# Output projection of two blocks at a time, FFN operands placed earlier, and 1/sqrt with its state in PSUM

## The chip, the cores and the metric

The kernel is one program on one core of a Trainium2 chip. The core has TensorE (matmuls, called PE in the profile, with its weight loads PEld), VectorE (DVE), ScalarE (ACT), GpSimd (POOL) and the DMA queues, which this kernel issues from SyncE (SP). The metric is the device time of one execution in microseconds; the median of three runs of the kernel before is 2169.43 us (2167.53 to 2169.79).

## The reference

One decoder layer on 2048 tokens of width 1024, in float32:

```
h    = rms_norm(x, norm1_g)
proj = h @ w_in                       # 1024 x 1536: u (512), xr (512), yr (512)
s5   = s5_mixer(u, ...)               # 32 groups, 64 complex states each, a scan over the sequence,
                                      # z = gelu(y);  z * sigmoid(z @ w_glu + b_glu)
lru  = rglru_mixer(xr, yr, ...)       # conv(4), gates, real scan, times gelu(yr)
mix  = concat(rms_norm(s5, s5_out_g), rms_norm(lru, lru_out_g))
x    = x + mix @ w_out                # 1024 x 1024
h2   = rms_norm(x, norm2_g)
x    = x + (silu(h2 @ w_gate) * (h2 @ w_up)) @ w_down     # 1024 x 2816 x 1024
out  = rms_norm(x, final_g)
```

## The kernel before

Tokens are cut into four blocks of 512 (`TB`, `NB`); features lie on partitions in chunks of 128. Every float32 product is made of three matmuls on rounded operands: an operand is split into `hi` (a cast on ACT) and `lo` (a subtraction on DVE or POOL), and `mm3` (line 214) accumulates hi x hi, hi x lo and lo x hi into one PSUM bank. A **unit** is 128 output columns of a projection: `Unit` loads its weights in parts of 128x512 into `wraw` (6 buffers) and splits them into `whi` (4 buffers) and `wlo` (5). A unit of eight chunks is 24 matmuls.

The stages, in the order of the work:

1. `in_tb(b)`, four times: the input projection of block b, its convolution, gates and real scan (the LRU group). The LRU output goes to DRAM (`lrud`, its 1/sqrt row to `rld`), the S5 input to `ub`.
2. S5, in two halves g of two blocks each: eight steps `s5_in`, `s5_scan`, `s5_out` a half on PE, DVE and POOL, through single `s_wr`, `s_wi`, `s_ta`, `s_tb` buffers, on the buffer `U` (tag `u8`), which goes to DRAM as `zb`.
3. `glu_tb(b)`: z of a block is loaded, GELU (`zgelu`), split into hi and lo (`zsplit`, lines 911 and 912), two units of 24 matmuls against `w_glu`, sigmoid and product, sum of squares, 1/sqrt (`SumSq.finish`, `rsqrt`, `spread`), and `mix`, which writes the normed and split operands of the output projection. The operands of even blocks lie in `areaH`, `areaL` (tiles `aH`, `aL`, pool Q), those of odd blocks in `actH`, `actL` (pool A). `zsplit` writes into the same places.
4. `out_tb(b)`: eight units against `w_out`; the sum with x (line 968), its square (ACT), the running sum of squares (POOL; DVE for block 3), the store to `x1d`; at the end a 1/sqrt row to `r2d`. The order is GLU 0, GLU 1, out 0, out 1, GLU 2, GLU 3, out 2, out 3.
5. The FFN in two halves p of two blocks, by a seven-product scheme over 2x2 blocks (`PRODS`). `combos(p, k)` loads two rows of `x1d` and the 1/sqrt row into the three `hx` buffers (lines 1053, 1055), norms them (line 1059) and forms four sums `ht`; `x_first(0)` splits them into the operand tiles, `LATE` ones through DRAM (`xcd`). Gate and up products are line 1184, the down projection line 1324. At the end the last norm.

**What sets the order.** The code gives each piece a time in the plan with `at(t, fn)`, in units near a microsecond (`PT` = 0.65 for three matmuls); `Plan.run` traces the pieces in the order of these times. The framework then gives each engine its instructions in an order in which operands are ready, earlier traced ones first, and a buffer is given again when its last reader is through. So a time in the plan is a priority, and buffers and readiness decide the rest. The pools lie one on the other: `open_d1` closes L, Q and S, and pool D1 (`hx`, `ht`, the operand tiles, `rd`, `ws`) takes their place; its first tiles, `hx`, lie where Q's `areaH` and `areaL` pieces lay. `open_d2` does the same with A and D2 behind the output projection.

**1/sqrt.** `rsqrt` (lines 221 to 236) takes four columns of sums and runs one scaling, two integer steps and three Newton rounds of three instructions, twelve DVE instructions on 128x4 elements, all in the SBUF tile `nv`. It runs 20 times: four times for the input norms, four for the LRU halves, four in GLU, four behind the output projection, four in the last norm. `aux("nm")` is a single PSUM bank.

Of the kernel before, what the change touches and what calls it, by code (L numbers as in the profile page):

```python
# [79 lines left out]
def build(tc, nc, I, O, ctx):  # L80
# [44 lines left out]
    x1d = dram("x1d", (DM, SEQ))  # L125
    r2d = dram("r2d", (SEQ,))
# [94 lines left out]
    def rsqrt(ss, n):  # L221

        w_ = ss.shape[-1]
        v = P.tile([128, 3, w_], F32, tag=f"nv{w_}", name="nv", bufs=2)
        ms, y, w = v[:, 0, :], v[:, 1, :], v[:, 2, :]
        DV.tensor_scalar(out=ms, in0=ss, scalar1=1.0 / n, scalar2=EPS, op0=ALU.mult, op1=ALU.add)

        DV.tensor_scalar(out=w.bitcast(I32), in0=ms.bitcast(I32), scalar1=1, scalar2=None, op0=ALU.logical_shift_right)
        DV.tensor_scalar(out=y.bitcast(I32), in0=w.bitcast(I32), scalar1=-1.0, scalar2=float(0x5F3759DF),
                         op0=ALU.mult, op1=ALU.add)  # L230
        for _ in range(3):
            DV.tensor_tensor(out=w, in0=y, in1=y, op=ALU.mult)
            DV.scalar_tensor_tensor(out=w, in0=w, scalar=-0.5, in1=ms, op0=ALU.mult, op1=ALU.mult)
            ins = DV.scalar_tensor_tensor(out=y, in0=w, scalar=1.5, in1=y, op0=ALU.add, op1=ALU.mult)
        last.setdefault("rs", getattr(ins, "ins", ins))
        return y

    class SumSq:
# [16 lines left out]
        def finish(self, dst=None):  # L255
# [4 lines left out]
            y = rsqrt(ps[:, 0:4], 128 * self.n)  # L260
# [3 lines left out]
        def spread(y, dst=None):  # L264
# [10 lines left out]
            dst = A.tile([128, TB], F32, tag="rs", name="rs", bufs=3)  # L275
# [334 lines left out]
    def in_tb(b, t0):  # L610
# [31 lines left out]
        at(ts + 9.0, lambda: cur.__setitem__("rs", SumSq.spread(rsqrt(cur["ss"], DM))))  # L642
# [225 lines left out]
    for g, (ts, dt) in enumerate(((ts0, 10), (tP1 - 10.0, 7))):  # L868
# [18 lines left out]
    def glu_tb(b, t0):  # L887
# [9 lines left out]
        def lload():  # L897
            cur["rl"] = lt("xq", (128, TB))
            cur["l"] = [lt("r", bufs=2) for _ in range(2)]
# [6 lines left out]

        def zsplit():
            zh, zl = pair(b)
# [10 lines left out]
        for uu in range(2):  # L919
# [3 lines left out]
            def prod(uu=uu, u=u):  # L923
                for i in range(2):
                    cur["ps", 2 * uu + i] = acc()
                    mm3(cur["ps", 2 * uu + i], u, [(4 * i + k, k) for k in range(4)],
                        *pair(b), True, True)
# [12 lines left out]
        t = t0 + 16 * PT  # L940

# [4 lines left out]
        for i, k in enumerate((4, 5, 6, 7)):  # L946
            at(max(t0 + 6.0, t2s) + 0.5 * i, lambda k=k: mix(k))
        at(t + 6.0, lambda: cur.__setitem__("rs", cur["ss"].finish()))
        for k in range(4):
            at(t + 7.0 + 0.5 * k, lambda k=k: mix(k))  # L950

    def out_tb(b, t0):
        cur = C[b]
        ss = SumSq(8, dv=b == NB - 1)
        for m in range(8):
# [572 lines left out]
```

## Time and profile before

| | us |
|---|---|
| median of three runs | 2169.43 (2167.53 to 2169.79) |
| profiled execution, its own time | 2175.18 |
| its span, first to last instruction | 2173.4 |
| TensorE busy | 1956.8 (90%) |
| DVE, POOL, ACT busy | 1244.8, 1042.6, 815.4 |
| last matmul of the output projection starts | 777.7 |
| first FFN matmul starts | 778.0 |

A row of a stretch reads: its bounds and length, then for each engine busy time and number of instructions, the granted TensorE clock, the share of the DMA engines and GB/s. A row of a group reads: line, engine, operation, out<-in, shapes, count, then busy time, mean ns of one, and idle time of the engine before it with what ended it. A wait reads: who waited for whom, total us, times, longest. A row of the timeline reads: start, length, engine, line, operation, count, and idle time before it. Matmuls overlap, so a row of one matmul is longer than its share of time. Some matmul records, a few per cent, can be missing.

### The profile page before, as it was taken

The numbers are of one execution on the slowest core, as the hardware profiler recorded it, in microseconds if no ns is written. First come the engines' busy times: TensorE is split into PE (matmuls) and PEld (weight loads), VectorE is DVE, ScalarE is ACT, GpSimd is POOL, SyncE is SP. The second block draws the span as 40 slices with busy tenths as digits, with TensorE's granted clock in tenths as the row PEclk, the third lists the DMA queues.
The fourth block names the chain that finished last, engine by engine and source line by source line (L and its number), as shares of the span: only waits on it lengthen the run. The fifth ranks groups of instructions, "written<-read, shape, count | busy, mean of one in ns | idle before, by whom it ended". The sixth has DMA issues, their size and how long they took to land.

```text
span 2173.4 us, 26158 instructions
## 1 busy us (share of the span) xinstructions
PE 1956.8 (90%) x8600; PEld 1564.3 (72%) x8600; DVE 1244.8 (57%) x1920; ACT 815.4 (38%) x1340; POOL 1042.6 (48%) x855
## 2 busy tenths in 40 slices
PE   6758989877898968899999989999999999999996
PEld 4536767666776756677777777777777788888785
DVE  5997658488856586444444464444444536554644
ACT  4534653563354342232332342232332344333331
POOL 1576236468834468545545552312313336544442
PEclk8968999988998989999999999999999999999998
DMA  7746998874772888644444574444443569854633
GB/s 293 218 153 190 297 248 273 226 179 142 226 209 94 257 264 279 200 146 146 160 146 143 172 235 134 149 131 136 145 131 126 189 224 317 279 184 135 232 102 102
DMA packets 264423, 413.61 MB, mean 190 GB/s; under 512 B 60736, under 2 KB 82528, under 8 KB 264288
## 3 DMA queue, kind: packets, MB, share of 16 engines
q1 hardware_dynamic: 264288, 411.95, 59.7%
q8 instruction: 67, 1.10, 0.2%
q14 instruction: 68, 0.56, 0.1%
HBM read 288.89 MB, written 122.96 MB: 189 GB/s over the span
## 4 chain that ended last, share of the span: by engine, by line
PE 55%; DVE 4%; DMA 4%; POOL 3%; issue 2%; ACT 1%; SPq 0%; POOLq 0%; DVEq 0%; ACTq 0%
PE gt L1184 9%; PE acc L1184 9%; PE y L1184 9%; PE v L1184 5%; PE nm L1184 5%; PE y L1324 4%; PE acc L1324 4%; PE gt L1324 4%; PE v L1324 2%; PE nm L1324 2%; PE acc L214 2%; DVE wlo L1024 1%; DMA ht<-xcd 1%; DVE hx L1059 1%; DMA wraw<-w_down 1%
## 5 line engine op out<-in xcount | busy, mean ns | idle before, releaser
L1197 POOL TENSOR_TENSOR t<-t 128x512 f32<-128x512 f32 x66 | 100.8, 1527 | 348.9 <-DVE t L1223 219.4
L214 PE MATMUL acc<-actH,whi 128*128 128x512 f32 x528 | 220.0, 418 | 43.5 <-DVE gy L710 12.1
L1023 ACT CAST whi<-ws 128x512 fp32r<-128x512 f32 x176 | 109.2, 621 | 346.9 <-PE y L1184 90.4
L214 PE MATMUL acc<-actL,whi 128*128 128x512 f32 x528 | 217.5, 413 | 18.8 <-DVE actL L294 17.8
L214 PE MATMUL acc<-actH,wlo 128*128 128x512 f32 x528 | 216.9, 412 | 6.9 <-DMA wlo<-wlc 6.9
L1024 DVE TENSOR_TENSOR wlo<-ht,whi 128x512 fp32r<-128x512 f32 x112 | 107.1, 957 | 126.3 <-ACT whi L1023 122.1
L214 PEld LDWEIGHTS acc<-actH,whi 128*128 128x128 f32 x528 | 105.9, 201 | 73.8 <-issue 24.8
L1023 ACT CAST whi<-ht 128x512 fp32r<-128x512 f32 x154 | 95.1, 619 | 169.9 <-PE nm L1324 69.5
L1024 DVE TENSOR_TENSOR wlo<-ws,whi 128x512 fp32r<-128x512 f32 x176 | 134.1, 762 | 33.7 <-ACT whi L1023 33.6
L1024 DVE TENSOR_TENSOR wlo<-wraw,whi 128x512 fp32r<-128x512 f32 x88 | 72.0, 818 | 142.2 <-ACT whi L1023 142.2
L1184 PE MATMUL y<-xh,whi 128*128 128x512 f32 x308 | 124.7, 405 | 16.2 <-ACT t L1216 12.0
L214 PEld LDWEIGHTS acc<-actL,whi 128*128 128x128 f32 x528 | 105.1, 199 | 46.7 <-DVE actL L294 24.7
L1024 POOL TENSOR_TENSOR wlo<-ht,whi 128x512 fp32r<-128x512 f32 x42 | 57.9, 1379 | 158.9 <-ACT whi L1023 158.9
L1184 PE MATMUL acc<-xh,wlo 128*128 128x512 f32 x308 | 122.3, 397 | 9.6 <-DVE wlo L1024 9.6
L214 PEld LDWEIGHTS acc<-actH,wlo 128*128 128x128 f32 x528 | 105.2, 199 | 30.6 <-DMA wlo<-wlc 7.4
L1184 PE MATMUL acc<-xh,whi 128*128 128x512 f32 x308 | 122.4, 397 | 4.6 <-ACT xh L1023 3.3
L1184 PE MATMUL y<-xl,whi 128*128 128x512 f32 x308 | 123.3, 400 | 3.5 <-DVE xl L1024 3.5
L1184 PE MATMUL y<-xh,wlo 128*128 128x512 f32 x308 | 123.3, 400 | 2.9 <-DVE wlo L1024 2.9
L1184 PE MATMUL acc<-xl,whi 128*128 128x512 f32 x308 | 122.2, 397 | 1.7 <-DVE xl L1024 1.7
L1184 PE MATMUL gt<-xh,whi 128*128 128x512 f32 x308 | 121.4, 394 | 0.0
L1184 PE MATMUL gt<-xh,wlo 128*128 128x512 f32 x308 | 121.3, 394 | 0.0
L1184 PE MATMUL gt<-xl,whi 128*128 128x512 f32 x308 | 121.2, 394 | 0.0
(416 smaller groups left out, 5308.0 us busy)
## 6 DMA issues: line engine op xcount, KB each, us to landing
td<-t SPq DMA_DIRECT2D x154, 256.0 KB, 2.2
ht<-td SPq DMA_DIRECT2D x154, 256.0 KB, 3.0
wraw<-w_down SPq DMA_DIRECT2D x99, 256.0 KB, 4.5
wraw<-w_in SPq DMA_DIRECT2D x96, 256.0 KB, 5.2
scd<-ws SPq DMA_DIRECT2D x88, 256.0 KB, 2.1
ws<-scd SPq DMA_DIRECT2D x88, 256.0 KB, 2.6
wlo<-wlc SPq DMA_DIRECT2D x72, 256.0 KB, 4.4
wraw<-w_out SPq DMA_DIRECT2D x64, 256.0 KB, 4.5
```

Source lines behind the costliest of these rows:

```text
L214: PE.matmul(ps, lhsT=part[w][:, kw % 4, :], rhs=r_(x(kx)), start=first and i == 0 and j == 0, stop=last and i == n - 1 and j == 2)
L1023: AC.copy(hi, raw)
L1024: eng.tensor_tensor(out=lo, in0=raw, in1=hi.bitcast(F32), op=ALU.subtract)
L1059: DV.scalar_tensor_tensor(out=cur[i], in0=cur[i], scalar=pc("g2", k + 4 * i), in1=cur["rs"], op0=ALU.mult, op1=ALU.mult)
L1184: PE.matmul(ps, lhsT=a[:, k, :], rhs=x, start=j in FIRST and k == 0 and i == 0, stop=k == 3 and i == 2, skip_group_check=True)
L1197: (DV if q == 0 else GP).tensor_tensor(out=g, in0=c, in1=g, op=ALU.mult)
L1324: PE.matmul(BK[p][i], lhsT=a[:, i, :], rhs=x, start=j in FIRST and s == 0 and v == 0, stop=s == NSL - 1 and v == 2, skip_group_check=True)
```

## The change

- **Pairs.** `out_pair(b0)` takes blocks 0 and 1 together, and then blocks 2 and 3: one `Unit` of weights serves both. Units go to the two `acc` and two `gt` banks in turn (`out_bank`). The order is (0,b0), (1,b0), (0,b0+1), (1,b0+1), then units 2 and up for both blocks in turn; for the first pair, units 6 and 7 come last, block 0 first, and 32 `PT` later in the plan.
- **GLU 2 and 3** are placed behind the first twelve units of pair 0, before its last four. Their z is split into a tile of tag `u8` (`zpair`) and no longer into the operand areas; all eight `mix` steps are placed by `tm`, behind units (7,0) and (7,1). Odd blocks load their LRU half into `ig` and `T` in place of `xq` and `r`.
- **S5's second half** is placed 16 later in the plan.
- **FFN operands.** `open_d1` and `x_first(0)` are placed 64 `PT` earlier, at the start of pair 2. `x1d` and `r2d` become two DRAM tiles each, one a pair.
- **Sums.** One running sum for each block of a pair (`sum`, `sumh`); block 2's additions go to DVE like block 3's; `rs` has two buffers in place of three.
- **1/sqrt.** Scaled sum, estimate and integer step live in the PSUM bank of the sums (`room`), one copy of the scaled sum and the temporary in SBUF; thirteen instructions in place of twelve, each with at most one input from SBUF. The input norm takes a bank `nm` for it.

```
--- before.py
+++ after.py
@@ -122,8 +122,8 @@
     kd = dram("kd", (NG, NCH, CT * NCH))
     md = dram("md", (128, 8, 4, 512))
     lrud = dram("lrud", (512, SEQ))
-    x1d = dram("x1d", (DM, SEQ))
-    r2d = dram("r2d", (SEQ,))
+    x1d = [dram(f"x1d{i}", (DM, 2 * TB)) for i in range(2)]
+    r2d = [dram(f"r2d{i}", (2 * TB,)) for i in range(2)]
     xcd = dram("xcd", (2, 4, 128, 7, TB))
     scd = dram("scd", (2, NSL, 4, 128, 4, 128))
     sdd = dram("sdd", (2, NSL, 128, 4, 128))
@@ -218,22 +218,24 @@
         return lambda k: t[:, k, :]
 
 
-    def rsqrt(ss, n):
+    def rsqrt(ss, n, room):
 
         w_ = ss.shape[-1]
+        mp, y, b = (room[:, (i + 1) * w_:(i + 2) * w_] for i in range(3))
         v = P.tile([128, 3, w_], F32, tag=f"nv{w_}", name="nv", bufs=2)
-        ms, y, w = v[:, 0, :], v[:, 1, :], v[:, 2, :]
-        DV.tensor_scalar(out=ms, in0=ss, scalar1=1.0 / n, scalar2=EPS, op0=ALU.mult, op1=ALU.add)
-
-        DV.tensor_scalar(out=w.bitcast(I32), in0=ms.bitcast(I32), scalar1=1, scalar2=None, op0=ALU.logical_shift_right)
-        DV.tensor_scalar(out=y.bitcast(I32), in0=w.bitcast(I32), scalar1=-1.0, scalar2=float(0x5F3759DF),
+        ms, w, r = v[:, 0, :], v[:, 1, :], v[:, 2, :]
+        DV.tensor_scalar(out=mp, in0=ss, scalar1=1.0 / n, scalar2=EPS, op0=ALU.mult, op1=ALU.add)
+
+        DV.tensor_scalar(out=b.bitcast(I32), in0=mp.bitcast(I32), scalar1=1, scalar2=None, op0=ALU.logical_shift_right)
+        DV.tensor_copy(out=ms, in_=mp)
+        DV.tensor_scalar(out=y.bitcast(I32), in0=b.bitcast(I32), scalar1=-1.0, scalar2=float(0x5F3759DF),
                          op0=ALU.mult, op1=ALU.add)
-        for _ in range(3):
-            DV.tensor_tensor(out=w, in0=y, in1=y, op=ALU.mult)
-            DV.scalar_tensor_tensor(out=w, in0=w, scalar=-0.5, in1=ms, op0=ALU.mult, op1=ALU.mult)
-            ins = DV.scalar_tensor_tensor(out=y, in0=w, scalar=1.5, in1=y, op0=ALU.add, op1=ALU.mult)
+        for i in range(3):
+            DV.scalar_tensor_tensor(out=w, in0=y, scalar=-0.5, in1=ms, op0=ALU.mult, op1=ALU.mult)
+            DV.tensor_tensor(out=w, in0=w, in1=y, op=ALU.mult)
+            ins = DV.scalar_tensor_tensor(out=r if i == 2 else y, in0=w, scalar=1.5, in1=y, op0=ALU.add, op1=ALU.mult)
         last.setdefault("rs", getattr(ins, "ins", ins))
-        return y
+        return r
 
     class SumSq:
 
@@ -257,7 +259,7 @@
             ps = aux("nm")
             for i in range(4):
                 PE.matmul(ps[:, i:i + 1], lhsT=self.s[:, 128 * i:128 * i + 128], rhs=ones, start=i == 0, stop=i == 3)
-            y = rsqrt(ps[:, 0:4], 128 * self.n)
+            y = rsqrt(ps[:, 0:4], 128 * self.n, ps)
             return self.spread(y, dst)
 
         @staticmethod
@@ -272,7 +274,7 @@
             for i in range(4):
                 PE.matmul(ps[:, 128 * i:128 * i + 128], lhsT=y[:, i:i + 1].to_broadcast([128, 128]), rhs=eye,
                           start=True, stop=True)
-            dst = A.tile([128, TB], F32, tag="rs", name="rs", bufs=3)
+            dst = A.tile([128, TB], F32, tag="rs", name="rs", bufs=2)
             AC.copy(dst, ps)
             return dst
 
@@ -639,7 +641,7 @@
         for i in range(4):
             at(ts + 2.5 * i - (9.0 if b == 0 else 5.0), lambda i=i: stat_load(i))
             at(ts + 2.5 * i, lambda i=i: stat(i))
-        at(ts + 9.0, lambda: cur.__setitem__("rs", SumSq.spread(rsqrt(cur["ss"], DM))))
+        at(ts + 9.0, lambda: cur.__setitem__("rs", SumSq.spread(rsqrt(cur["ss"], DM, aux("nm")))))
 
         def evac_u(m):
             us = v_us[:, m % 2, :]
@@ -865,7 +867,7 @@
             AC.copy(U.rearrange("p (q l) c -> p q l c", l=2)[:, :, gl, :],
                     Y[gl][:, 0:2 * NS].rearrange("p (q c) -> p q c", q=2))
 
-    for g, (ts, dt) in enumerate(((ts0, 10), (tP1 - 10.0, 7))):
+    for g, (ts, dt) in enumerate(((ts0, 10), (tP1 + 6.0, 7))):
         for half in range(2):
             at(ts - 3.0 + 2 * dt * half, lambda g=g, half=half: s5_u(g, half))
             at(ts + 10.0 + dt * (4 * half + 3), lambda g=g, half=half: s5_z(g, half))
@@ -884,7 +886,8 @@
     def pair(b):
         return (areaH, areaL) if b % 2 == 0 else (chunks_of(actH), chunks_of(actL))
 
-    def glu_tb(b, t0):
+    def glu_tb(b, t0, tm=None):
+
         cur = C[b] = {}
 
         def zload():
@@ -895,8 +898,8 @@
                              zb[b // 2, :, 8 * j:8 * j + 8, :, o:o + CB].rearrange("t g h c -> (g h) t c"))
 
         def lload():
-            cur["rl"] = lt("xq", (128, TB))
-            cur["l"] = [lt("r", bufs=2) for _ in range(2)]
+            cur["rl"] = lt("xq" if b % 2 == 0 else "ig", (128, TB))
+            cur["l"] = [lt("rT"[b % 2], bufs=2) for _ in range(2)]
             SP.dma_start(cur["rl"], rld[b].unsqueeze(0).to_broadcast([128, TB]))
             for h in range(2):
                 SP.dma_start(cur["l"][h], lrud[256 * h:256 * h + 256, b * TB:(b + 1) * TB].rearrange("(j p) t -> p j t", j=2))
@@ -904,8 +907,16 @@
         def zgelu():
             act(out=cur["z"], in_=cur["z"], func=AF.Gelu_apprx_tanh)
 
+        def zpair():
+            if b < 2:
+                return pair(b)
+            if "zhl" not in cur:
+                zz = bt("u8", (128, 2, 4, TB))
+                cur["zhl"] = tuple((lambda k, i=i: zz[:, i, k, :]) for i in range(2))
+            return cur["zhl"]
+
         def zsplit():
-            zh, zl = pair(b)
+            zh, zl = zpair()
             z = cur["z"]
             for j in range(4):
                 AC.copy(r_(zh(j)), z[:, j, :])
@@ -924,7 +935,7 @@
                 for i in range(2):
                     cur["ps", 2 * uu + i] = acc()
                     mm3(cur["ps", 2 * uu + i], u, [(4 * i + k, k) for k in range(4)],
-                        *pair(b), True, True)
+                        *zpair(), True, True)
 
             at(t, prod)
 
@@ -938,53 +949,68 @@
 
             at(t + 8 * PT + 0.5, post)
         t = t0 + 16 * PT
+        tm = t + 7.0 if tm is None else tm
 
         def mix(k):
             src, rs = (cur["z"][:, k, :], cur["rs"]) if k < 4 else (cur["l"][k // 2 - 2][:, k % 2, :], cur["rl"])
             norm_split(k, src, pc("gm", k), rs, *pair(b), eng=GP if k % 2 else DV)
 
         for i, k in enumerate((4, 5, 6, 7)):
-            at(max(t0 + 6.0, t2s) + 0.5 * i, lambda k=k: mix(k))
+            at((max(t0 + 6.0, t2s) if b < 2 else tm - 2.0) + 0.5 * i, lambda k=k: mix(k))
         at(t + 6.0, lambda: cur.__setitem__("rs", cur["ss"].finish()))
         for k in range(4):
-            at(t + 7.0 + 0.5 * k, lambda k=k: mix(k))
-
-    def out_tb(b, t0):
-        cur = C[b]
-        ss = SumSq(8, dv=b == NB - 1)
-        for m in range(8):
-            t = t0 + m * 8 * PT
-            u = Unit(t, I["w_out"][m], 8, GP if m % 3 == 1 else DV)
-
-            def prod(m=m, u=u):
-                cur["o", m] = acc()
+            at(tm + 0.5 * k, lambda k=k: mix(k))
+
+    def out_bank():
+        n = last["bank"] = last.get("bank", -1) + 1
+        return acc() if n % 4 < 2 else aux("gt", 2)
+
+    def out_pair(b0, t0):
+
+
+
+
+        sums = {b: SumSq(8, ("sum", "sumh")[b % 2], dv=b >= NB - 2) for b in (b0, b0 + 1)}
+        blocks = (b0, b0 + 1)
+        order = [(m, b) for b in blocks for m in (0, 1)]
+        order += [(m, b) for m in range(2, 6 if b0 == 0 else 8) for b in blocks]
+        if b0 == 0:
+            order += [(m, b) for b in blocks for m in (6, 7)]
+        units = {}
+        for n, (m, b) in enumerate(order):
+            cur = C[b]
+            t = t0 + n * 8 * PT + (32 * PT if b0 == 0 and n >= 12 else 0)
+            if m not in units:
+                units[m] = Unit(t, I["w_out"][m], 8, GP if m % 3 == 1 else DV)
+
+            def prod(m=m, b=b, cur=cur, u=units[m]):
+                cur["o", m] = out_bank()
                 mm3(cur["o", m], u, [(k, k) for k in range(8)], *pair(b), True, True)
 
-            at(t - 5, lambda m=m: cur.__setitem__(("x", m), load_chunk(xT, b, m)))
-            at(t, prod)
-
-            def post(m=m):
+            def post(m=m, b=b, cur=cur):
                 xc = cur.pop(("x", m))
                 DV.tensor_tensor(out=xc, in0=cur.pop(("o", m)), in1=xc, op=ALU.add)
-                ss.add(xc)
-                SP.dma_start(x1d[128 * m:128 * m + 128, b * TB:(b + 1) * TB], xc)
-
+                sums[b].add(xc)
+                SP.dma_start(x1d[b // 2][128 * m:128 * m + 128, TB * (b % 2):TB * (b % 2) + TB], xc)
+
+            at(t - 5, lambda m=m, b=b, cur=cur: cur.__setitem__(("x", m), load_chunk(xT, b, m)))
+            at(t, prod)
             at(t + 8 * PT + 0.5, post)
-
-        def fin():
-            ss.finish(r2d[b * TB:(b + 1) * TB])
-
-        at(t0 + 64 * PT + 4.0, fin)
+            if m == 7:
+                at(t + 8 * PT + 4.0, lambda b=b: sums[b].finish(r2d[b // 2][TB * (b % 2):TB * (b % 2) + TB]))
 
     glu_tb(0, tin[3] + 64 * PT + 5.3)
     T = tP1 + 16 * PT
-    for kind, b in (("g", 1), ("o", 0), ("o", 1), ("g", 2), ("g", 3), ("o", 2), ("o", 3)):
-        if kind == "g":
-            glu_tb(b, T)
-            T += 16 * PT
-        else:
-            out_tb(b, T)
-            T += 64 * PT
+    glu_tb(1, T)
+    T += 16 * PT
+    out_pair(0, T)
+
+    tg = T + 96 * PT
+    glu_tb(2, tg, T + (128 + 16 + 1) * PT)
+    glu_tb(3, tg + 16 * PT, T + (128 + 32 + 1) * PT)
+    T += 128 * PT + 32 * PT
+    out_pair(2, T)
+    T += 128 * PT
     tC = T
 
 
@@ -1044,15 +1070,14 @@
 
     def combos(p, k, t):
 
-        o = 2 * TB * p
         cur = {}
 
         def load():
             for i in range(2):
                 cur[i] = d1("hx", 3, w=2 * TB)
-                SP.dma_start(cur[i], x1d[128 * (k + 4 * i):128 * (k + 4 * i) + 128, o:o + 2 * TB])
+                SP.dma_start(cur[i], x1d[p][128 * (k + 4 * i):128 * (k + 4 * i) + 128])
             rs = cur["rs"] = d1("hx", 3, w=2 * TB)
-            SP.dma_start(rs, r2d[o:o + 2 * TB].unsqueeze(0).to_broadcast([128, 2 * TB]))
+            SP.dma_start(rs, r2d[p].unsqueeze(0).to_broadcast([128, 2 * TB]))
 
         def norm():
             for i in range(2):
@@ -1327,8 +1352,8 @@
         def load_row(q, p, i):
 
             x = tmp()
-            m, o = i + 4 * (q // 2), TB * (2 * p + q % 2)
-            SP.dma_start(x, x1d[128 * m:128 * m + 128, o:o + TB])
+            m, o = i + 4 * (q // 2), TB * (q % 2)
+            SP.dma_start(x, x1d[p][128 * m:128 * m + 128, o:o + TB])
             return x
 
         def row_tile(p, q, i):
@@ -1375,7 +1400,7 @@
             ps = bank(f"d{p}", TAGS_D if p else TAGS_G)
             for i in range(4):
                 PE.matmul(ps[:, i:i + 1], lhsT=s[:, 128 * i:128 * i + 128], rhs=ones, start=i == 0, stop=i == 3)
-            y = rsqrt(ps[:, 0:4], DM)
+            y = rsqrt(ps[:, 0:4], DM, ps)
             ps = bank(f"d{p}", TAGS_D if p else TAGS_G)
             for i in range(4):
                 PE.matmul(ps[:, 128 * i:128 * i + 128], lhsT=y[:, i:i + 1].to_broadcast([128, 128]), rhs=eye,
@@ -1429,9 +1454,9 @@
                     T += QD
     tD = T
 
-    at(tC - 64 * PT + 4.0, open_d1)
+    at(tC - 128 * PT + 4.0, open_d1)
     at(tC + 1.0, open_d2)
-    x_first(0, tC - 64 * PT + 12.0)
+    x_first(0, tC - 128 * PT + 12.0)
     x_load(0, {j: gt[0, 0, 0, j] for j in LATE})
     x_ahead(1, [gt[0, 3 + 2 * k, 0, 1] for k in range(4)])
     x_load(1, {j: gt[1, 0, 0, j] for j in PRODS})
```

## The prediction

> **What bounds the kernel now.** I read the page first, then stretches of the span, then single queues. The page says that TensorE is the busy engine:
>
> ```profile
> span 2173.4 us, 26158 instructions
> PE 1956.8 (90%) x8600; PEld 1564.3 (72%) x8600; DVE 1244.8 (57%) x1920; ACT 815.4 (38%) x1340; POOL 1042.6 (48%) x855
> ```
>
> So time can be won only where TensorE is not fed. The stretches below cut the part that the change touches (columns: PE, PEld, DVE, ACT, POOL busy with instructions, then granted clock, DMA share, GB/s):
>
> ```profile
> 443.00:507.00 64.00, 53.55 (x297) 42.88 (x298) 57.59 (x90) 32.91 (x51) 52.16 (x60) 0.89 0.54 154
> 507.00:584.00 77.00, 62.75 (x307) 48.80 (x306) 67.17 (x111) 23.88 (x47) 66.05 (x86) 0.93 0.68 209
> 584.00:640.00 56.00, 52.36 (x235) 43.53 (x236) 30.83 (x50) 28.95 (x49) 28.39 (x22) 0.94 0.74 205
> 640.00:687.00 47.00, 37.59 (x159) 29.11 (x158) 33.29 (x61) 20.65 (x35) 22.03 (x16) 0.85 0.29 92
> 687.00:727.00 40.00, 40.00 (x175) 32.08 (x174) 16.09 (x23) 16.41 (x27) 17.38 (x13) 1.00 0.59 178
> 727.00:778.00 51.00, 47.22 (x205) 38.22 (x204) 41.68 (x49) 19.38 (x34) 30.61 (x19) 0.97 0.88 292
> ```
>
> These are, in order: the tail of the input projection with GLU 0 and 1; output block 0 beside the second S5 half; output block 1; GLU 2 and 3; output block 2; output block 3. Of the same stretches, the 128x512 matmuls of the projections alone (line 214), and those of the FFN (line 1184) behind them:
>
> ```profile
> 443.00:507.00 64.00, 37.90 (x145) 27.98 (x146) 0.89 0.54 154
> 507.00:584.00 77.00, 51.09 (x193) 37.08 (x192) 0.93 0.68 209
> 584.00:640.00 56.00, 45.11 (x193) 36.04 (x194) 0.94 0.74 205
> 640.00:687.00 47.00, 32.87 (x117) 23.29 (x116) 0.85 0.29 92
> 687.00:727.00 40.00, 39.99 (x172) 32.08 (x173) 1.00 0.59 178
> 727.00:778.00 51.00, 46.26 (x194) 36.93 (x192) 0.97 0.88 292
> ```
>
> ```profile
> 778.00:900.00 122.00, 85.27 (x321) 63.92 (x321) 0.86 0.78 257
> ```
>
> In 687:727 nothing is missing (clock 1.00), so a fed matmul costs 39.99 / 172 = 0.2325 us, a unit of 24 costs 5.6, a GLU block of 48 costs 11.2. The small matmuls (all others of a stretch) I put at 0.1 us. What a stretch lost is its length less these: 64 - 33.7 - 15.2 = 15; 77 - 44.9 - 11.4 = 21; 56 - 44.9 - 4.2 = 7; 47 - 27.2 - 4.2 = 16; 0; 51 - 45.1 - 1.1 = 5. In the FFN's start 122 - 321 x 0.2325 = 47. Slow clock behind idle time is inside these numbers. So 64 us are lost before 778 and 47 behind it; the change works on both.
>
> What ended TensorE's waits in 443:690 (total, times, longest):
>
> ```profile
> PE acc L214 <- DVE xc L968: 10.0, 4, 4.3
> PE acc L214 <- ACT aH L300: 6.8, 3, 4.4
> PE nm L273 <- DVE nv L234: 6.3, 2, 5.1
> ```
>
> The first is an output unit that waits for one of two PSUM banks, the second a new block's operands, the third a 1/sqrt.
>
> **Part 1: pairs of blocks.** Half of 16 x 4 weight parts disappear: 32 loads, 32 casts and 32 subtractions. Their prices stand in 420:830:
>
> ```profile
> L188 ACT CAST whi<-wraw 128x512 fp32r<-128x512 f32 x79 | 47.8, 615 | 39.6 <-PE acc L214 27.8 <-DMA wraw<-w_out 6.5 <-issue 2.9
> L189 POOL TENSOR_TENSOR wlo<-wraw,whi 128x512 fp32r<-128x512 f32 x32 | 47.2, 1477 | 30.4 <-ACT whi L188 29.6 <-POOL ht L1070 0.5
> L189 DVE TENSOR_TENSOR wlo<-wraw,whi 128x512 fp32r<-128x512 f32 x47 | 41.6, 887 | 28.9 <-ACT whi L188 24.9 <-DMA wraw<-w_out 2.6 <-issue 1.3
> ```
>
> ACT loses 32 x 0.615 = 20 us, DVE 20 x 0.887 = 18, POOL 12 x 1.477 = 18. None lies on TensorE's path by itself; it takes load from DVE and POOL, which are busy 67 and 66 of 77 us in 507:584. Four PSUM banks in turn in place of two remove most of the 10.0 us. GLU 2 and 3, whose stretch loses 16, get output units of blocks 0 and 1 around them, and the later blocks' z goes into S5's freed buffer, so it no longer waits for an operand area. Block 2's operands are written under units (6,1) and (7,1).
>
> How early can pair 2 start? Two limits. Fed without a gap from 507, TensorE has 16 units (89), two GLU blocks (22) and 156 small matmuls (16): 127 us, pair 2 at 634. The other limit is S5, which GLU 2 needs whole:
>
> ```profile
> 443.35 0.90 PE L801 MATMUL v<-u,mi 128*64 128x128 f32 x8 [2.25 <-DMA u<-ub]
> 618.31 1.92 ACT L150 ACTIVATE zA<-zA 128x2048 f32<-128x2048 f32 x1
> 639.85 0.39 PE L214 MATMUL acc<-aH,whi 128*128 128x512 f32 x1
> ```
>
> S5's second half starts at 443 as soon as its input has landed, and the GELU of block 2's z ends at 620; GLU 2 starts 20 us later, and this slack is now asked for. Twelve pair units from 507 (67 + 16 us, and 10 lost) are through at 600, so GLU 2 waits. Its two weight units take the four `whi` buffers ahead of units 6 and 7, so these can't fill the hole. Then follow 22 for GLU 2 and 3, 22 for four units, some 7 of splits and mixing: pair 2 at 672. Moving S5's events by 16 us of the plan puts them behind GLU 1 and the first loads on SP, DVE and POOL, yet both engines have less to do. I take the middle, 653. Today block 2 starts, without loss, at 687 - 20 matmuls = 682. **Gain 30, from 10 to 48.** Block 3's lost 5 us shrink to 3: gain 2, from 0 to 5. One `rs` buffer fewer costs nothing as long as a block's mix is over before the second next 1/sqrt, which pair units now separate; if not, a GLU block's mix waits for the one before, some 6 us once. The seven square sums of block 2 go from POOL to DVE, which has the room (16.09 of 40 busy in 687:727); without it they are 7 more DVE additions of about the 0.89 of a weight split, 6 us. The LRU halves of odd blocks load into other buffers and are no longer held by the even block; the 32 stores and 16 loads of `x1d` stay.
>
> **Part 2: FFN operands.** The plan moves them 41.6 of its us earlier, with 12 loads and 8 stores on SP. But pool D1 lies where pool Q was, and its first tiles, the three `hx` buffers, lie on block 2's operands:
>
> ```profile
> 727.00 0.39 PE L214 MATMUL acc<-aH,wlo 128*128 128x512 f32 x1
> 727.69 0.90 SPq L1053 DMA_DIRECT2D hx<-x1d  x2
> 729.25 0.79 SPq L1055 DMA_DIRECT2D hx<-r2d  x1
> 737.33 2.48 DVE L1059 SCALAR_TENSOR_TENSOR hx<-hx,par 128x1024 f32<-128x1024 f32 x2 [3.15 <-DMA hx<-r2d]
> 744.57 1.72 POOL ht L1070
> ...
> DMA to landing us min/median/max: 2.0/5.1/7.3
> ...
> 795.43 2.48 DVE L1059 SCALAR_TENSOR_TENSOR hx<-hx,par 128x1024 f32<-128x1024 f32 x2
> ```
>
> Today the first load leaves 0.7 us behind the last matmul on `aH`, and output block 3 (51 us) covers what follows. In the pair the last reader of `aH` is unit (7,2), the last but one: the cover shrinks to one unit, 5.6 us. From `aH` free (727.4) to the FFN's start without loss (900 - 74.6 = 825.4) are 98 us now. If all 98 stay, the FFN loses 98 - 5.6 = 92 instead of 47: cost 45. But today's four `hx` steps (737.33 to 795.43, 19.4 each) share DVE with block 3 (41.7 of 51 busy). Alone, a step is 2.5 (norm), 6.5 (from its end at 739.8 to that of the fourth sum, 746.3, when a `hx` buffer comes free) and the landing of the next load, 5.1 to 7.3, say 6.5: 15.5. Three steps with 10 for the first load and 5 to the first product make 61.5; with no further loss the cost is 61.5 - 5.6 - 47 = 9. The first FFN weights, and the operands of p = 1, still press in behind. I take 79: **cost 26, from 9 to 45.** The other queues lose their cover too: `rd` and `ws` weight tiles lie in D1, but these need less time than four `hx` steps.
>
> **Part 3: Newton steps.** Twelve instructions become thirteen, none with two SBUF inputs. Duration min/median/max:
>
> ```profile
> L232 DVE TENSOR_TENSOR nv<-nv x60: 130/162/2336, 42.5 to 2160.7; 128x4 f32<-128x4 f32 x60
> L226 DVE TENSOR_SCALAR nv<-nm x12: 128/154/160, 188.6 to 793.2; 128x4 f32<-128x4 f32 x12
> L806 DVE TENSOR_TENSOR s_wr<-v,mi x16: 393/424/425, 289.4 to 578.5; 128x256 f32<-128x256 f32 x16
> L843 DVE TENSOR_TENSOR s_wr<-s_tb,mi x16: 393/416/1497, 294.0 to 585.0; 128x256 f32<-128x256 f32 x16
> ```
>
> The same multiplication never exceeds 425 ns with an input from PSUM (`v`), and reaches 1497 with both from SBUF. So the long ones should go. What they cost:
>
> ```profile
> L232 DVE TENSOR_TENSOR nv<-nv 128x4 f32<-128x4 f32 x60 | 20.1, 342 | 1.3
> L234 DVE SCALAR_TENSOR_TENSOR nv<-nv 128x4 f32<-128x4 f32 x60 | 15.6, 267 | 1.3
> L233 DVE SCALAR_TENSOR_TENSOR nv<-nv 128x4 f32<-128x4 f32 x60 | 14.4, 246 | 1.2
> L228 DVE TENSOR_SCALAR nv<-nv 128x4 int32<-128x4 int32 x20 | 8.0, 407 | 0.3
> ```
>
> 58.1 us, against 200 x 0.16 = 32: 26 too many over 20 calls, 1.3 each. Those in the output stage are inside part 1. Seven calls (four input norms, three of the LRU halves) lie before 443, 9 us, partly where DVE is the bound:
>
> ```profile
> 100.00:200.00 100.00, 58.25 (x227) 42.99 (x228) 99.87 (x140) 39.80 (x58) 72.85 (x64) 0.75 0.50 162
> ```
>
> I take **a gain of 5, from -1 to 9**; the end is a thirteenth instruction of 0.16 us on the last 1/sqrt. A write to PSUM is shown by no row: between 0.13 (the least `nv`) and 0.42 us (`L806`), and I take 0.16, as of the PSUM read. [...]
>
> **Sum.** -30 - 2 + 26 - 5 = -11. On the profiled execution (2175.18, span 2173.4 and 1.8 around it) that is 2164; the median of the runs is 5.75 lower, 2169.43, so I predict **2158 us**.
>
> **Rivals.** (a) Slower: S5 decides. If block 2's z is ready no earlier than 620 and GLU 2's weights hold the `whi` buffers, pair 2 starts at 672 (gain 10), and the FFN start costs 35 while DVE is as crowded as now: -10 - 2 - 5 + 35 = +18, 2187. It decides from pair 2 at about 663, where 19 + 7 of gain meet a cost of 26. For it: S5 took 177 us from 443 to 620 with a place 16 us further ahead in the plan; against: the freed 18 us on each of DVE and POOL. (b) The operands do get early, the change does what its name says: the `hx` steps run under pair 2, and of the 47 lost at the FFN's start some 20 remain: -30 - 2 - 5 - 27 = -64, 2105. Against it speaks the load that leaves right behind the last matmul on `aH`. (c) Both sides cancel: the gain is 20 since DVE and POOL, not TensorE, pace 507:584: -20 - 2 - 5 + 26 = -1, 2168.
>
> **Chances.** Forecast (2140 to 2164) 0.40, (a) 0.38, (b) 0.12, (c) 0.10. 0.2% is 4.3 us, about what a measurement of this kernel can tell from no change. Faster is the forecast and (b), 0.52; same 0.10; slower 0.38. The range must hold most of (a) and half of (b): 2108 to 2190; of the forecast alone, from gain and cost at their chosen halves, 2140 to 2164.
>
> **What would show it.** Part 1: output matmuls waiting for `xc` near 0, no stretch with a clock of 0.85 between GLU 2 and pair 2, first matmul of pair 2 between 634 and 672. Rival (a): TensorE idle ahead of GLU 2 until the GELU on `zA`. Part 2: the first `hx` load behind the last but one output unit, and then some 70 us in which TensorE is idle or slow; if loads of `hx` stand in the middle of pair 2, (b) holds and I am wrong by some 50 us. Part 3: no Newton instruction above 0.45 us.

## The result, and the profile after

The changed kernel takes 2196.27 us, median of four runs (2192.26 to 2199.47); beside it the kernel before took 2169.61 (2167.53 to 2171.63). The ratio is 1.0122, 95% interval 1.0103 to 1.0141: **26.7 us slower**, where 11 us faster was predicted. The profiled executions, 2196.63 and 2175.18, are 21.4 apart, and the traces are to explain these 21.4 (the profiled execution of before lies 5.6 above the median of its runs, that of after 0.4). The page of the kernel after:

```profile
span 2194.9 us, 25988 instructions
PE 1964.2 (89%) x8600; PEld 1564.3 (71%) x8600; DVE 1207.0 (55%) x1927; ACT 802.2 (37%) x1308; POOL 1016.9 (46%) x836
```

DVE lost 38 us of work, POOL 26, ACT 13, as the change says, and the kernel is slower. Two points in the trace divide the difference. The first is the last output matmul and the FFN behind it (timeline of TensorE; stretch of line 1209 alone, the FFN's matmuls; TensorE's waits):

```profile
767.75 0.39 PE L214 MATMUL gt<-actH,wlo 128*128 128x512 f32 x1
```

```profile
768.00:900.00 132.00, 68.99 (x230) 47.99 (x230) 0.72 0.72 241
```

```profile
PE acc L1209 <- DVE wlo L1050: 10.3, 1, 10.3
```

The output stage ends at 768.0, 10 us earlier than before (778.0). By 900 the FFN has done 230 matmuls against 321, so it starts, without loss, at 900 - 230 x 0.2325 = 846.5 against 825.4. The FFN's start loses 78.5 us where it lost 47: 31 more. -10 + 31 = +21, the whole difference; the wait of 10.3 near 900 has its twin of 9.6 before and is no part of it.

The second is inside the output stage. Matmuls of line 214 alone, in four stretches, first before, then after:

```profile
507.00:560.00 53.00, 35.59 (x130) 25.55 (x130) 0.90 0.69 213
560.00:614.00 54.00, 36.30 (x151) 27.75 (x150) 0.94 0.68 203
614.00:640.00 26.00, 24.32 (x108) 19.82 (x107) 1.00 0.76 203
640.00:690.00 50.00, 35.85 (x130) 25.73 (x129) 0.86 0.27 87
```

```profile
507.00:560.00 53.00, 17.67 (x64) 11.24 (x64) 0.87 0.66 184
560.00:614.00 54.00, 51.14 (x220) 41.08 (x220) 1.00 0.65 177
614.00:640.00 26.00, 21.34 (x72) 15.12 (x72) 0.87 0.32 98
640.00:690.00 50.00, 43.62 (x177) 32.53 (x178) 1.00 0.28 90
```

In 507:560 the changed kernel does 66 matmuls fewer, 15 us of work; in 560:614 it runs full (220 in 54 us) and only catches up; 614:640 falls short again. What stands in 507:560, from the waits of 443:690 and the timeline of TensorE:

```profile
PE y L864 <- POOL s_s L854: 6.9, 3, 2.6
PE nm L275 <- DVE nv L236: 6.1, 1, 6.1
PE acc L214 <- POOL aL L303: 4.9, 5, 2.4
```

```profile
526.08 0.95 PE L261 MATMUL nm<-ones,sumg 128*128 128x1 f32 x8
544.02 2.05 PE L275 MATMUL nm<-eye,nv 128*128 128x128 f32 x8 [6.13 <-DVE nv L236]
552.50 0.50 PE L214 MATMUL gt<-actL,whi 128*128 128x512 f32 x1 [1.86 <-DVE actL L303]
614.06 0.74 PE L214 MATMUL acc<-u,whi 128*128 128x512 f32 x2 [1.18 <-ACT u L922]
```

The waits for `xc` are gone. In their place TensorE waits for block 1's operands: its GLU's square sum leaves TensorE at 526, the 1/sqrt is back at 544 through DVE and POOL busy with S5, and the units on `actH` run from 552. The pairs want these operands as the third unit; before, they were wanted as the ninth. The last row is GLU 2, behind the GELU on `zA` (ACT):

```profile
611.07 1.92 ACT L150 ACTIVATE zA<-zA 128x2048 f32<-128x2048 f32 x1
```

At the FFN's start the timeline of SP, DVE and POOL shows:

```profile
758.51 2.88 SPq L1078 DMA_DIRECT2D hx<-x1d  x2
```

```profile
768.78 2.62 DVE L1084 SCALAR_TENSOR_TENSOR hx<-hx,par 128x1024 f32<-128x1024 f32 x2
776.48 1.64 DVE L1094 TENSOR_TENSOR ht<-ht,hx 128x512 f32<-128x512 f32 x1
789.93 0.17 DVE L227 TENSOR_SCALAR nm<-nm 128x4 f32<-128x4 f32 x1 [3.04 <-PE nm L261]
792.20 2.48 DVE L1084 SCALAR_TENSOR_TENSOR hx<-hx,par 128x1024 f32<-128x1024 f32 x2
798.15 0.69 DVE L1094 TENSOR_TENSOR ht<-ht,hx 128x512 f32<-128x512 f32 x1
805.17 2.48 DVE L1084 SCALAR_TENSOR_TENSOR hx<-hx,par 128x1024 f32<-128x1024 f32 x2 [4.05 <-DMA hx<-r2d]
818.50 2.48 DVE L1084 SCALAR_TENSOR_TENSOR hx<-hx,par 128x1024 f32<-128x1024 f32 x2 [4.42 <-DMA hx<-r2d]
```

```profile
777.53 1.74 POOL L1166 TENSOR_TENSOR ws<-wraw,ws 128x512 f32<-128x512 f32 x1
779.22 1.75 POOL L1166 TENSOR_TENSOR ws<-wraw,rd 128x512 f32<-128x512 f32 x1
780.90 1.73 POOL L1095 TENSOR_TENSOR ht<-hx,ht 128x512 f32<-128x512 f32 x1
```

The two loads leave at 758.5 and 761.1, while the last but one output unit runs (756.9 to 762.5); SyncE's queue waits for this unit's matmuls (waits of SP in 755:763):

```profile
SPq L1078 <- PE gt L214: 2.7, 2, 2.4
```

The first step from norm to norm takes 23.4 us, the next two 13.0 and 13.3. In the first, the fourth sum stands on POOL behind two sums of FFN weights (`ws`) and starts 12.1 us behind its norm (780.90), where the second step's starts 6.8 behind (798.99). The second norm stands on DVE behind block 3's 1/sqrt; TensorE forms that block's sum only at 787.97, behind block 2's 1/sqrt. Before, FFN weight sums and block 3's 1/sqrt lay in the third step, which took 21.4 us (774.08 to 795.43):

```profile
774.08 4.57 DVE L1059 SCALAR_TENSOR_TENSOR hx<-hx,par 128x1024 f32<-128x1024 f32 x2
793.16 0.16 DVE L226 TENSOR_SCALAR nv<-nm 128x4 f32<-128x4 f32 x1 [1.96 <-PE nm L259]
```

Three of the four norms started ahead of the end of the output stage then (737.33, 755.20 and 774.08, with the end at 778.0). Now all four start behind it (768.78 and later, with the end at 768.0).

### The profile page after: what moved, and what is told of

It reads as the page before. It is cut to its first block, busy times and chain, and to the rows that moved or that the text cites. A ratio compares the mean times of both kernels' runs of the same rounds, so it can differ in the third digit from the quotient of the medians.

```text
span 2194.9 us, 25988 instructions
## 1 busy us (share of the span) xinstructions
PE 1964.2 (89%) x8600; PEld 1564.3 (71%) x8600; DVE 1207.0 (55%) x1927; ACT 802.2 (37%) x1308; POOL 1016.9 (46%) x836
## 4 chain that ended last, share of the span: by engine, by line
PE 67%; DVE 13%; DMA 7%; POOL 5%; ACT 3%; issue 3%; SPq 1%; POOLq 0%; DVEq 0%; ACTq 0%
PE acc L1209 9%; PE gt L1209 9%; PE y L1209 9%; PE acc L214 8%; PE v L1209 5%; PE nm L1209 5%; PE acc L1349 4%; PE y L1349 4%; PE gt L1349 4%; PE gt L214 3%; PE nm L1349 2%; PE v L1349 2%; POOL s_s L854 1%; DMA ht<-xcd 1%; DMA wraw<-w_in 1%
## 5 line engine op out<-in xcount | busy, mean ns | idle before, releaser
L214 PE MATMUL acc<-actH,whi 128*128 128x512 f32 x424 | 177.8, 421 | 43.1 <-DVE gy L712 14.8
L214 PE MATMUL acc<-actL,whi 128*128 128x512 f32 x424 | 177.3, 418 | 17.8 <-DVE actL L296 16.5
L214 PE MATMUL acc<-actH,wlo 128*128 128x512 f32 x424 | 174.9, 413 | 2.3 <-DMA wlo<-wlc 2.0
L1209 PE MATMUL acc<-xh,wlo 128*128 128x512 f32 x308 | 123.8, 402 | 10.3 <-DVE wlo L1050 10.3
L214 PEld LDWEIGHTS acc<-actH,whi 128*128 128x128 f32 x424 | 85.0, 201 | 67.3 <-issue 24.1
L214 PEld LDWEIGHTS acc<-actL,whi 128*128 128x128 f32 x424 | 85.3, 201 | 40.6 <-DVE actL L296 22.7
L1049 ACT CAST whi<-wraw 128x512 fp32r<-128x512 f32 x88 | 54.6, 621 | 159.6 <-PE y L1209 53.0
```

The source lines that it names most:

```text
L214: PE.matmul(ps, lhsT=part[w][:, kw % 4, :], rhs=r_(x(kx)), start=first and i == 0 and j == 0, stop=last and i == n - 1 and j == 2)
L1049: AC.copy(hi, raw)
L1209: PE.matmul(ps, lhsT=a[:, k, :], rhs=x, start=j in FIRST and k == 0 and i == 0, stop=k == 3 and i == 2, skip_group_check=True)
```

## The experiments

All ratios are to the kernel before, run beside each kernel, with 95% intervals. The medians of before lie between 2169.61 and 2173.39 in the four sets of runs, so runs of different sets are compared by their ratios. "Output end" is the start of the last line-214 matmul and 0.23; "FFN at" is 900 less 0.2325 for each FFN matmul started before 900; "lost between" is the second less the first. The edits of the order are shown in a shorter form than the kernels have. The kernels:

| run | ratio | output end | FFN at | lost between |
|---|---|---|---|---|
| before (profiled execution) | 1 | 778.0 | 825.4 | 47 |
| after | 1.0122 [1.0103, 1.0141] | 768.0 | 846.5 | 78.5 |
| 1 Newton steps alone | 0.9969 [0.9953, 0.9985] | 770.3 | 820.0 | 50 |
| 2 four banks alone | 1.0005 [0.9989, 1.0021] | 778.7 | 825.8 | 47 |
| 3 blocks 2, 3 in turn | 0.9977 [0.9961, 0.9993] | 771.4 | 820.3 | 49 |
| 4 two units of cover | 1.0078 [1.0052, 1.0103] | 769.4 | 845.4 | 76 |
| 5 all blocks in turn | 0.9896 [0.9875, 0.9918] | 765.2 | 804.0 | 39 |
| 6 and S5 at its old place | 0.9883 [0.9861, 0.9905] | 758.1 | 796.5 | 38 |
| 7 pairs, light S5 | 1.0073 [1.0053, 1.0092] | 760.0 | 842.8 | 83 |
| 8 four units of cover | 1.0065 [1.0044, 1.0086] | 780.1 | 841.9 | (62) |
| 9 pairs, S5 at its old place | 1.0066 [1.0053, 1.0078] | 762.7 | 844.7 | 82 |
| 10 in turn, light S5 | 0.9903 [0.9888, 0.9918] | 752.6 | 802.4 | 50 |
| 11 pairs, old Newton | 1.0116 [1.0102, 1.0129] | 768.1 | 846.5 | 78 |
| 12 as 6, two banks | 0.9850 [0.9837, 0.9864] | 762.2 | 798.2 | 36 |

Most of them have the wait of TensorE near 900, and it ends ahead of 900; but in after it ends at 900.4 and in run 11 at 902.5, so run 11's FFN stands some 2 us too early in this table.

**1. Newton steps alone** (the new `rsqrt` and its PSUM `room` in the kernel before; the edit is that function as the change's diff has it, and its three calls).

> The kernel before with the Newton steps of 1/sqrt in PSUM alone (thirteen instructions, each with at most one operand from SBUF), nothing else of the change. The prediction's third part: 5 us faster, from 1 slower to 9 faster, 2164 us. Rival: the 26 us of long Newton instructions were time in which DVE waited for POOL anyway and lie off TensorE's path; then the time is that of before within 2 us, 2168 to 2171. [...]

Measured 2165.83, by the ratio 6.7 us faster (3 to 10). The prediction's third part holds. The gain is in the output stage, which ends 7.7 us earlier; z comes 14 us earlier (618.31 before):

```profile
604.66 1.91 ACT L150 ACTIVATE zA<-zA 128x2048 f32<-128x2048 f32 x1
```

**2. Four banks alone.**

```diff
-                cur["o", m] = acc()
+                cur["o", m] = out_bank()
```

> The kernel before with four PSUM banks in turn for the output units in place of two, nothing else of the change. Theory, as in the prediction: TensorE's 10.0 us of waits for xc in 443 to 690 go, and most of it comes off the end: 2160 to 2164 us. Rival: the waits only move, since GLU 2 cannot start before the S5 half is through (z ready at 620) and block 1's units have slack until then: 2166 to 2170.

Measured 2173.62, ratio 1.0005: no change, as the rival forecast. The 10.0 us of waits for `xc` are gone, but TensorE stands longer elsewhere: its waits for the 1/sqrt rise from 6.3 to 9.6, and those for S5 (`mo`, `s_s`) from 4.0 to 7.9.

```profile
PE nm L273 <- DVE nv L234: 9.6, 3, 5.1
```

The rival's reason does not hold: z of block 2 is ready at 613.4, and GLU 2 starts only at 637.1, right behind block 1's last unit.

**3. Blocks 2 and 3 in turn** (pair 0 as in the change; the second edit, in all kernels with another order, loads a unit's weights again when its last use lies more than three units back).

```diff
+        if b0 == 2:
+            order = [(m, b) for b in blocks for m in range(8)]
...
-            if m not in units:
+            if m not in [x[0] for x in order[max(0, n - 3):n]]:
```

> The kernel after, but the second pair done as two blocks in turn: all eight units of block 2, then all eight of block 3, each unit's weights loaded and split twice. The first pair, the Newton steps and the early place of the FFN operands stay. Theory, lost cover: the first hx load leaves behind block 2's last unit, some 45 us ahead of the end of the output stage, the FFN's start loses 47 us again in place of 78, and the time is 2196 - 31 = 2165 us. Rival, crowding: the FFN's start is paced by DVE and POOL splits and by the weights whatever lies ahead of it; it gains at most 8 from cover, 2188 or more.

Measured 2167.83; against after, by the ratios, -1.45% or 31 us, as the cover theory forecast. In the trace the FFN's start loses 49 us in place of 78.5. The first norm stands at 732.57 instead of 768.78, and the FFN has 343 matmuls by 900:

```profile
732.57 2.48 DVE L1084 SCALAR_TENSOR_TENSOR hx<-hx,par 128x1024 f32<-128x1024 f32 x2 [4.36 <-DMA hx<-r2d]
```

```profile
771.00:900.00 129.00, 93.90 (x343) 70.83 (x344) 0.83 0.75 252
```

The second pair itself wins 3.4 us of the output stage (768.0 against 771.4).

**4. and 8. Two and four units of cover** (the order of pair 2's end: e is 6 in run 4; in run 8 it is 4 for the second pair, and four weight units are loaded and split twice).

```diff
-        order += [(m, b) for m in range(2, 6 if b0 == 0 else 8) for b in blocks]
-        if b0 == 0:
-            order += [(m, b) for b in blocks for m in (6, 7)]
+        order += [(m, b) for m in range(2, e) for b in blocks]
+        order += [(m, b) for b in blocks for m in range(e, 8)]
```

> The kernel after with the last four units of the second pair in the order (6,2) (7,2) (6,3) (7,3) in place of (6,2) (6,3) (7,2) (7,3), as the first pair ends already: two units of block 3 behind block 2's last one in place of one. Theory, lost cover: one unit more of cover, 5.6 us off the FFN's start, 2190 us. Rival, crowding: no change, 2194 to 2198.

> The kernel after with the second pair's end in the order (4 to 7, block 2), (4 to 7, block 3), the four weight units loaded and split twice: four units of block 3 behind block 2's last one, 22.4 us of cover in place of 5.6. Theory, lost cover, with the chain from the last matmul on block 2's operands to the FFN's start growing from 84 to some 89 us as more of it runs beside output units: the FFN's start loses 67 in place of 78, 2185 us. Rival, a fixed start of the FFN: no change, 2194 to 2198.

Measured 2188.45 and 2185.80, near both forecasts of the cover theory. The traces show less: the FFN starts 1.1 and 4.6 us earlier than in after, where 5.6 and 11 were forecast. (Run 4's profiled execution, 2195.80, is the slowest of its six.) So run 3 carries the cover theory, and these two point the same way. The first `hx` load leaves at 753.49 and 747.22:

```profile
753.49 2.89 SPq L1078 DMA_DIRECT2D hx<-x1d  x2
```

```profile
747.22 0.90 SPq L1078 DMA_DIRECT2D hx<-x1d  x2
```

From load to the FFN's start are 88.0 us after, 91.9 and 94.7 here, and 95.8 in run 3 (load at 724.5). Of the 5.0, 11.3 and 34.0 us by which the load leaves earlier, 1.1, 4.6 and 26.2 reach the FFN's start: the chain takes longer where more of it runs beside output units. In run 8 the last output units run behind the FFN's first matmuls (769.4, with the output end at 780.1), so its 62 is not to be compared.

**5. and 6. All blocks in turn, then S5 at its old place** (the second edit in run 6 alone).

```diff
+        order = [(m, b) for b in blocks for m in range(8)]
...
-    for g, (ts, dt) in enumerate(((ts0, 10), (tP1 + 6.0, 7))):
+    for g, (ts, dt) in enumerate(((ts0, 10), (tP1 - 10.0, 7))):
```

> The kernel after with all four blocks in turn: block 0's eight output units, four of block 1, GLU 2 and 3, the other four of block 1, then blocks 2 and 3; each unit's weights are loaded and split twice. Four banks, Newton steps in PSUM, the later S5 half and z in the freed S5 buffer stay. Theory, order of the first pair: in the pairs block 1's operands are wanted at the third unit instead of the ninth, TensorE stands there while DVE and POOL work on S5, and by 550 it is 50 output-stage matmuls (11.6 us) behind before. In turn, the count by 550 is back at about 1345, but z of block 2 is ready no earlier than about 612 and takes most of it back: 0 to 5 us faster than with only blocks 2 and 3 in turn (2168 us), 2163 to 2168. Rival, weights: splitting them twice costs DVE and POOL the time that S5 needs; 2172 us or more.

> As the kernel with all four blocks in turn, with S5's second half at its old place in the plan (16 us earlier). Theory: with the order of the first pair undone, S5 is what GLU 2 waits for; its old place brings z of block 2 some 8 us earlier and the time 3 to 8 us lower than without, 2158 to 2163. Rival: S5 is held by DVE and POOL and not by its place; no change within 2 us.

Measured 2149.79 and 2146.23, both far below their forecasts. The order theory of run 5 is right in place and size: 507:560 has 134 matmuls, where run 3 has 67, and z takes most of it back, GLU 2 waiting 5 us for it; the output stage ends 6.2 us earlier than in run 3.

```profile
507.00:560.00 53.00, 37.01 (x134) 25.75 (x133) 0.94 0.78 230
```

```profile
611.62 1.65 PE L214 MATMUL acc<-u,whi 128*128 128x512 f32 x3 [4.99 <-ACT u L922]
```

(The first row is line 214's stretch, the second TensorE's timeline.) The other 10 us of run 5 nobody had forecast: TensorE's wait near 900, 9.6 before and 10.3 after, isn't there. In run 3 (8.0 us at 871.7) it is the next norm on DVE, waiting for its load, ahead of a weight split that TensorE needs:

```profile
867.50 2.48 DVE L1084 SCALAR_TENSOR_TENSOR hx<-hx,par 128x1024 f32<-128x1024 f32 x2 [8.85 <-DMA hx<-r2d]
```

In runs 5, 6 and 12 TensorE's longest wait between 820 and 905 is 2.7 to 3.6 us. Why the order comes out better there was not tried. In run 6 z comes 7.8 us earlier than in run 5, as forecast, and the output stage ends 7.1 us earlier; the ratios show 3 us of it, inside both intervals.

**7. and 10. Light S5**, in the changed kernel and in the one with all blocks in turn (S5's place as after). The second half's carry, scans and the four multiplications behind them are left out.

```diff
-        if g == 0:
+        if g == 0 or g == 1:
             GP.memset(sv[:, :, :, 0:1], 0.0)
...
-        for q in range(2):
+        for q in range(2 if g == 0 else 0):
...
+        if g == 1:
+            ta, tb_ = wi, wr
+        else:
...
```

> The kernel after with S5's second half made light: of each of its eight steps the carry from the first half, the four scans and the four multiplications behind them are left out (the output is no longer the reference's); TensorE's and ACT's work, the loads and the order stay. Theory: what holds the output stage from 505 to 615 is DVE and POOL busy with S5, so that block 1's operands and z of block 2 come late; with S5 light the count by 550 rises by 30 or more, the second pair's start moves from 679 to about 660, and the time falls by 15 to 20, 2176 to 2181 us. Rival: the output stage's own chain (GLU, 1/sqrt, mix) paces it; less than 5 us, 2191 or more.

> The kernel with all four blocks in turn (S5's place as after) and the light S5 of the seventh run together; S5's carries, scans and the multiplications behind them are left out for its second half. Theory: order and S5 are the two limits of the part ahead of pair 2; with both gone the output stage ends some 12 us ahead of the one in turn alone (765.0), at about 753, and the time is about 2138. Rival: behind z a third limit, the chain GLU 2 and 3, 1/sqrt, mix, keeps block 2's start within 5 us of 670: 2145 or more.

Run 7: 2187.99, 0.5% or 11 us below after, between the two forecasts. 507:560 has 115 matmuls instead of 64, and the output stage ends 8 us earlier: the second pair starts, without loss, at 670.7, where 660 was forecast. Run 10: the output end, 752.6, is the 753 forecast; the time, 2151.54, isn't 2138, because the wait near 900 is back (7.3) and the start of the FFN loses 50, where run 5 lost 39.

```profile
507.00:560.00 53.00, 32.34 (x115) 23.29 (x116) 0.87 0.73 209
```

```profile
507.00:560.00 53.00, 41.27 (x160) 29.63 (x158) 0.98 0.82 242
```

```profile
598.61 1.22 PE L214 MATMUL acc<-u,whi 128*128 128x512 f32 x2 [3.81 <-ACT u L925]
```

The last two rows are of run 10: 160 matmuls in 507:560, the most of all runs, and GLU 2 at 598.6. Block 2 starts, without loss, at 663.3 (752.6 less 384 x 0.2325): 65 us from GLU 2 to the next block, as after (614.1 to 678.7). With GLU 2 15 us earlier that chain is no shorter: it is a limit of its own.

**9. The changed kernel with S5 at its old place.**

> The kernel after with S5's second half at its old place in the plan, nothing else changed. Theory, two limits that meet: in the kernel after the first twelve pair units end at 613 and the GELU of block 2's z at 613; an earlier S5 brings z to about 605 but not the twelve units, so the output stage gains 0 to 3 us: 2192 to 2198. Rival, S5 alone decides (as from the fifth to the sixth run, where the output stage ended 7 us earlier): 2187 to 2190.

Measured 2187.39, inside the rival's range, and 5.3 us in the output stage: more than the 0 to 3 of the theory. But S5 alone doesn't decide either: z is 18.5 us earlier, and the twelve pair units end at 611, where they end at 613 in after (line 214's 507:560 still has 68). GLU 2 then starts without a wait, and its first 24 matmuls, which take 8.4 us in after, waiting for the splits of z, run in 5.7.

```profile
592.52 1.92 ACT L150 ACTIVATE zA<-zA 128x2048 f32<-128x2048 f32 x1
```

```profile
507.00:560.00 53.00, 21.57 (x68) 14.58 (x69) 0.78 0.65 181
```

So the later place of S5 is a loss by itself: 6.6 us between the profiled spans, 0.56% or 12 us between the ratios.

**11. The changed kernel with the old Newton steps.**

> The kernel after with the Newton steps as before (twelve instructions in SBUF, two operands from it). Theory: the PSUM form is worth in the changed kernel what it was worth alone, 7 us: 2203. Rival: with weights halved DVE and POOL collide less, and it is worth nothing here: 2196.

Measured 2198.84, ratio 1.0116 against 1.0122: nearer the rival. By the ratios the new steps lose 1 us here, by the profiled spans (2197.1 and 2194.9) they win 2; by the intervals a gain of up to some 4 us is not excluded. So most of the 7 us that they were worth alone is gone behind the pairs, although the old form's waits are there:

```profile
PE nm L273 <- DVE nv L234: 12.7, 2, 8.9
```

With the old form GLU 2 even starts 3.3 us earlier (610.8), yet the output stage ends at the same time. Why was not tried.

**12. As run 6, with two banks.**

> The kernel with all four blocks in turn and S5 at its old place (2146 us), with two PSUM banks for the output units in place of four. Theory, as for the banks alone: units that wait for a bank are ahead of S5 anyway; no change, 2143 to 2149. Rival: with the order and S5 mended, waits for xc lie on the path again and the two banks cost 4 to 10 us, 2150 to 2156.

Measured 2141.52, the best of all: 1.5% (32 us) faster than before. Waits for `xc` are 1.3 us in all; four banks win nothing here either. By the ratios two are 0.3% better, with intervals that just overlap; in the traces the output stage ends 4 us later than in run 6, and the FFN is at 798.2 against 796.5.

```profile
PE acc L214 <- DVE xc L992: 1.3, 1, 1.3
```

## Why the prediction was wrong

**Part 1, the step that failed.** "I take the middle, 653" gave a gain of 30 + 2, and with the Newton steps' 5 the part ahead of the FFN was to win 37. The output stage ends 10 us earlier, with either form of the Newton steps (778.0 to 768.0 and 768.1). Pair 2's first matmul is at 670.3. Counted from its first part, as the prediction counted block 2 (58 matmuls by 690), it starts without loss at 676.5 against 682: a gain of 6 and not 30. Inside blocks 2 and 3 another 4 us are won, where 2 were forecast; counted back from the output end, the start without loss is 678.7. Four things were wrong behind the middle:
- Its early end, "fed without a gap", needed block 1's operands at the third unit. The prediction counted what the pairs remove and never asked when the units' operands are wanted. That costs 15 us in 507:560 (run 5 against run 3), of which 6 are left at the end of the output stage, and the twelve units were through at 613 instead of 600.
- S5's later place was waved through since "both engines have less to do". Run 9 shows 18.5 us of z for it, 5 us of output stage.
- The tail from GLU 2 to pair 2 was put at 22 + 22 + 7 = 51; it took 56 to pair 2's first matmul and 65 to its start without loss, and 65 again in run 10.
- Four banks "remove most of the 10.0 us": the wait goes, the time doesn't (runs 2 and 12). The 20, 18 and 18 us of weight work that disappear lay off TensorE's path, as the prediction said; the three fastest kernels (runs 5, 6 and 12) load and split weights twice.

What was right: no waits for `xc`; and the limit of S5 and the `whi` buffers, 672, lay close to the first matmul at 670.3. That was partly luck: z came 7 us earlier than assumed, and the way from there took 57 us and not 51. Rival (a) asked for TensorE idle ahead of GLU 2 until the GELU, and there it stood 1.2 us only: in the changed kernel the units and z come due together. The granted clock between GLU 2 and pair 2 did fall, to 0.87 in 614:640, where the prediction wanted no such stretch.

**Part 2 was right.** Cost 26 forecast, 31 measured; from `aH` free (762.5) to the FFN's start 84 us, where 79 was taken between 61.5 and 98. The `hx` loads did leave with the last but one output unit, though while it ran and not behind it. A step alone takes 13.0 to 13.3 and not 15.5; the first takes 23.4, because FFN weight sums and the 1/sqrt of blocks 2 and 3 lie in it. Before, such work lengthened a step too (21.4), but the two steps ahead of it ran beside block 3's units. In both kernels the first loads leave when block 2's operands come free; what the earlier place in the plan does by itself no run shows. That `hx` in space free of block 2's operands would give rival (b)'s gain was not tried. Nor were the z tile, the two `rs` buffers, block 2's sums on DVE and the new places of the LRU halves run alone.

**Part 3 was right alone** (5 forecast, 6.7 measured) and worth little or nothing in the sum, where it was added as if independent: run 11. Its price for an instruction was right. None of the Newton instructions of the kernel after is above 0.17 us (duration min/median/max in ns):

```profile
L234 DVE SCALAR_TENSOR_TENSOR nv<-nm,nv x48: 130/161/163, 42.9 to 791.9; 128x4 f32<-128x4 f32 x48
L235 DVE TENSOR_TENSOR nv<-nv,nm x48: 127/157/159, 43.1 to 792.1; 128x4 f32<-128x4 f32 x48
L236 DVE SCALAR_TENSOR_TENSOR nm<-nv,nm x32: 150/166/167, 43.3 to 791.7; 128x4 f32<-128x4 f32 x32
```

With its output in PSUM an instruction takes 0.166 us (median), in SBUF 0.157 to 0.161. The multiplication with one input from PSUM has a median of 0.157 (`L235`), the old one, all in SBUF, of 0.162 (`L232` of before).

**The sum.** -30 - 2 - 5 + 26 = -11 became -10 + 31 = +21 in the traces: of the 32 us between them 27 are the output stage and 5 the FFN's start. With part 2 as forecast the sign hung on the output stage alone, and the prediction had put the point of decision at a pair 2 that starts at 663; it started at 670 to 679. Rival (a) gave 2187, 9 us short of the median.

## What to carry to other kernels

When two blocks share a weight, the second block's operands are wanted earlier (here six units earlier). Look first for what makes those operands (here a 1/sqrt behind S5), and for what reads the space of the next stage last (here the block whose cover shrank from 51 us to 5.6). Loads, splits and bank waits that go away off the path brought nothing here. A gain measured alone need not be there beside another change in the same stretch: run the sum with the part taken out, as in run 11.

## What the runs showed of the hardware

The same 128x512 operation of DVE on two SBUF operands took 1.64 us at 776.48, in a stretch where POOL works without a break, and 0.69 at 798.15, where POOL stood idle (797.49 to 798.99). At 777 to 783 POOL starts an instruction every 1.69 us and the DVE instructions on two SBUF operands take as long (1.68 to 1.74), each starting 0.54 to 0.60 us behind one of POOL's. This is part of why the first `hx` step is longer than the others: block 2's 1/sqrt, from 771.33 to 786.90, stands among eight DVE instructions on two SBUF operands of 1.64 to 1.78 us each. The instructions of that 1/sqrt, with at most one operand from SBUF, took 0.14 to 0.17 us.
